# Four input projections of a hybrid convolution and linear-attention block computed as seven products of half-size blocks

## The chip, the cores and the metric

The kernel runs on one core of one Trainium2 chip. The metric is the device time of one execution in microseconds (us). A core has five engines with a queue of their own each: TensorE (PE in the profile, with its weight loads in a row of their own, PEld), VectorE (DVE), ScalarE (ACT), GpSimd (POOL) and SyncE (SP). An engine works its queue off in order. In this kernel SP issues the loads of weights and inputs, and POOL issues the small constants and everything that goes to scratch memory in DRAM and back.

## The reference

512 tokens of width 2048 pass through one layer. Only the part before the output projection is changed.

```python
u = rmsnorm(x, norm1_g)
z = u @ w_in                      # 2048 x 6160
cb, cc, ch, q, k, v, og, a_low = split(z)   # 1024 x3, 512 x2, 1024 x2, 16 columns
y_conv = group_rms(cb * causal_conv3(cc * ch)) * conv_g
log_a  = log_sigmoid(a_low @ w_gate_up + b_gate) / 16
o      = gla_chunk_causal(q, k, v, log_a)   # chunks of 64 tokens, 4 heads
y_gla  = rms(o) * gla_g * silu(og)
x = x + concat(y_conv, y_gla) @ w_out
x = x + relu(rmsnorm(x) @ w_ff1)**2 @ w_ff2
out = rmsnorm(x)
```

## The kernel before

All weights arrive in float32. For a matmul each operand is split into two rounded parts, hi and lo (ACT copies the hi part, DVE subtracts to get the lo part), and a product is the sum of three matmuls: hi by hi, hi by lo, lo by hi (`mm3`). A unit of weights is 512 KB (128 partitions by 1024 elements): SP loads it into one of four `raw` buffers, ACT makes `hi` (three buffers) and DVE makes `lo` (three buffers).

The front half runs in this order. `project_v(0)` computes half of v, 512 columns wide, token by token (`token_major`, the activations as stationary operand), while x, transposed, is loaded and split into `u` tile by tile; the square sums for the norm come from a second load of x. Two products of 264 columns (`tm_t`) give the gate's low-rank input and k. `project_v(1)` follows, with the decay gates between its matmuls, then eight products for the out-gate (`fm_og`), four for q (`fm_q`), and eight groups of the convolution, each with three products of 128 features by 512 tokens: cc, ch and cb (`fm_cc`, `fm_ch`, `fm_cb`, one call of `feature_major` each, 48 matmuls of 512 columns). The linear attention is written as a generator, `gla(h)`: a hook in `feature_major` takes one step of it after every third matmul. One chunk is a matmul `kv`, a VectorE update of the state `st`, four steps of nothing and then two matmuls `o`. A head runs in one of every two convolution groups, in its first two products.

After the front come the output projection (`tm_op`) and the two feed-forward products (`f1...` and `f...`). These two are already computed by seven products of half-size blocks: of four weight blocks `block_forms` makes seven forms by additions on DVE, each is split into hi and lo, and each product is 24 matmuls of 256 columns. A tile framework orders the instructions of each engine by a cost model of its own, and places all waits.

Of the kernel before, what the change touches and what calls it, by code (L numbers as in the profile page):

```python
# [8 lines left out]
F32 = mybir.dt.float32  # L9
# [25 lines left out]

Q0, K0, V0, O0, A0 = 3072, 3584, 4096, 5120, 6144
# [3 lines left out]
def hymba_kernel(  # L40
    ctx, tc, x, x_t, w_tok0, w_tok, w_feat, w_gate, conv_w, conv_g, g1, g2, gla_g, gf,
# [92 lines left out]
    nc.gpsimd.dma_start(glag, gla_g)  # L134
    r1 = const_tile("r1", [P, NT])
# [51 lines left out]

    u = []
    w_ready = []
    yt = [None] * KT  # L190
    with tc.tile_pool(name="mix", bufs=1) as mix:
# [4 lines left out]

        xq = [wide(f"xt_{k}", ("og0", "og1", "vv1", "kk")[k]) for k in range(4)]

        def load_u(e):
            k = 2 * e  # L200
            part = xq[k // 4][:, k % 4 : k % 4 + 2, :]
            nc.sync.dma_start(part, x_t[:, k : k + 2, :])
            for m in range(2):
                u.append(split_scaled(part[:, m, :], g1t[:, k + m : k + m + 1], "u", k + m))

        def load_first(kt):
            part = xq[0][:, kt, :]
            nc.sync.dma_start(part, x_t[:, kt, :])
            u.append(split_scaled(part, g1t[:, kt : kt + 1], "u", kt))


        ss1 = mix.tile([P, NT], F32, name="ss1", tag="ss1")
        a1 = mix.tile([P, NT], F32, name="a1", tag="a1")
        def square_sum(i):
            xi = mix.tile([P, D], F32, name=f"x_{i}", tag="yr", bufs=2)
            nc.sync.dma_start(xi, x[i * P : (i + 1) * P, :])
            S.activation(xi, xi, AF.Square, accum_out=ss1[:, i : i + 1])

        vv = [None, None]
        def project_v(n, hook, before=None):  # L220
            def put(i, b):
                if i == 0:
                    vv[n] = wide(f"vv_{n}", f"vv{n}")
                S.activation(vv[n][:, i, :], b, AF.Copy, scale=r1[:, i : i + 1])

            token_major(u, w_tok, 8 * n, 8, 512, 2, f"v{n}", put, hook, before)

        def start(j):
            if j < 7:
                load_u(j + 1)  # L230
            if 4 <= j <= 7:
                square_sum(j - 4)
            if j == 7:
                mean_eps(a1, ss1, D)
                rsqrt_of(r1, a1, mix, "r1")

        project_v(0, start, load_first)
# [10 lines left out]
        r1sb = mix.tile([P, SEQ], F32, name="r1sb", tag="r1sb")  # L248
        eab = mix.tile([P, SEQ], F32, name="eab", tag="eab")

        def along_free(dst, col, factor, name):
            b = bank(f"{name}_ps", "aux")
            for i in range(NT):
                d = mix.tile([P, P], F32, name=f"{name}_d{i}", tag="diag", bufs=1)
                V.tensor_scalar_mul(d, ident, col[:, i : i + 1])
                T.matmul(b[:, i * P : (i + 1) * P], onesg, d, start=True, stop=True)
            S.activation(dst, b, AF.Copy, scale=factor)


        alow = mix.tile([P, NT, RANK], F32, name="alow", tag="alow")  # L260
        kk = wide("kk", "kk")

        def put0(i, b):
            S.activation(alow[:, i, :], b[:, :RANK], AF.Copy, scale=r1[:, i : i + 1])
            V.tensor_scalar_mul(kk[:, i, 0:248], b[:, RANK:264], r1[:, i : i + 1])

        def put1(i, b):
            S.activation(kk[:, i, 248:512], b[:, :264], AF.Copy, scale=r1[:, i : i + 1])

        token_major(u, w_tok0, 0, 4, 264, 4, "t0", put0)  # L270
        along_free(r1b, r1, float(P), "r1b")
        along_free(eab, a1, float(P) * EPS, "eab")
        V.tensor_tensor(out=r1sb, in0=r1b, in1=r1b, op=ALU.mult)
        token_major(u, w_tok0, 4, 4, 264, 4, "t1", put1)

        kd = [kk, wide("kk_odd", "kk2")]
        G.memset(kd[1][:CHUNK], 0.0)
        al3 = mix.tile([P, NT, 96], F32R, name="al3", tag="al3")  # L280
# [33 lines left out]
        def gate_decay(i):  # L314
# [6 lines left out]
            V.tensor_tensor(out=kd[1][CHUNK:, i, :], in0=kk[CHUNK:, i, :], in1=t[CHUNK:], op=ALU.mult)  # L321
            V.tensor_tensor(out=kk[:CHUNK, i, :], in0=kk[:CHUNK, i, :], in1=t[:CHUNK], op=ALU.mult)
# [10 lines left out]
        def gates(j):  # L333
            if j == 0:
                gate_alt()
            if 1 <= j <= 2:
                gate_in(2 * j - 2)
                gate_in(2 * j - 1)
            if j == 2:
                gate_log()  # L340
            if 5 <= j <= 6:
                gate_decay(2 * j - 10)
                gate_decay(2 * j - 9)

        project_v(1, gates)


        og = [wide(f"og_{n}", f"og{n}") for n in range(2)]
        for k in range(8):
            b = feature_major(w_feat[HEADS + k], u, f"og{k}")  # L350
            t = mix.tile([P, SEQ], F32, name=f"ogt_{k}", tag=f"hs{k % 2}")
            V.tensor_tensor(out=t, in0=b, in1=r1b, op=ALU.mult)
            S.activation(og[k // 4][:, k % 4, :], t, AF.Silu)
        qt = []
        for h in range(HEADS):
            b = feature_major(w_feat[h], u, f"q{h}")
            q = mix.tile([P, SEQ], F32, name=f"q_{h}", tag=f"q{h}")
            V.scalar_tensor_tensor(
                out=q, in0=b, scalar=float(DK) ** -0.5, in1=r1b, op0=ALU.mult, op1=ALU.mult
            )  # L360
            qt.append(q)

        def gla(h):
# [3 lines left out]
            cv = slice(h % 2 * DV, (h % 2 + 1) * DV)  # L367
            for c in range(NCHUNK):
# [3 lines left out]
                    kv[:, :DV], kd[c % 2][:, i, h * DK : (h + 1) * DK], vv[h // 2][:, i, cv],  # L372
# [13 lines left out]
                for d in range(2):  # L386
                    T.matmul(
                        o[d][:, t], st[:, d * P : (d + 1) * P], qt[h][:, t], start=True, stop=True,
                        skip_group_check=True,
                    )  # L390
# [10 lines left out]
            mean_eps(a, m, 2.0)  # L401
# [15 lines left out]
        def conv(j, hook, hook_last):  # L417
            if j % 4 == 0:
                yraw.append(wide(f"y_{j}", "yr", bufs=2))
            b = feature_major(w_feat[12 + 3 * j], u, f"cc{j}", hook)  # L420
            cc = mix.tile([P, SEQ], F32, name=f"cc_{j}", tag="cc")
            V.tensor_tensor(out=cc, in0=b, in1=r1sb, op=ALU.mult)
            b = feature_major(w_feat[13 + 3 * j], u, f"ch{j}", hook)
# [5 lines left out]
            V.tensor_scalar_mul(cv, up[:, 0:SEQ], w(0))  # L429
# [4 lines left out]
            b = feature_major(w_feat[14 + 3 * j], u, f"cb{j}", hook_last)  # L434
            V.tensor_tensor(out=cv, in0=b, in1=cv, op=ALU.mult)
# [30 lines left out]

        norm = None
        for j in range(NG):
            steps = gla(j // 2) if j % 2 == 0 else iter(())
            pending = [norm]  # L470

            def hook(kt):
                if kt == 8 and pending[0]:
                    pending.pop()()
                    pending.append(None)
                next(steps, None)

            norm = conv(j, hook, y_last if j == NG - 1 else hook)
            for _ in steps:
                pass  # L480
        norm()
        y_conv(NG - 1)

# [5 lines left out]

    wt = ctx.enter_context(tc.tile_pool(name="wt", bufs=1, reuse_waits="tile"))  # L490

    def load_quarters(src, i0, n, name):

        raws = []
        for q in range(4):
            raw = wp.tile([P, UNIT], F32, name=f"raw_{name}{q}", tag="raw", bufs=RAWS)
            nc.sync.dma_start(raw[:, :n], src[i0 + q])
            raws.append(raw[:, :n])
        return raws

    def split_w(src, n, name):
        hi = wp.tile([P, UNIT], F32R, name=f"hi_{name}", tag="hi", bufs=3)
        lo = wp.tile([P, UNIT], F32R, name=f"lo_{name}", tag="lo", bufs=3)
        S.copy(hi[:, :n], src)  # L504
        V.tensor_tensor(out=lo[:, :n], in0=src, in1=hi[:, :n].bitcast(F32), op=ALU.subtract)  # L505
        return hi, lo

    def plus(in0, in1, n, name, into=None):
        w = into
        if w is None:  # L510
            w = wt.tile([P, 1024], F32, name=f"w_{name}", tag="w", bufs=2)[:, :n]
        V.tensor_tensor(out=w, in0=in0, in1=in1, op=ALU.add)  # L512
        return w

    def block_forms(src, i0, n, name):

        b12, b11, b21, b22 = load_quarters(src, i0, n, name)
        w = {}

        def parts_of(f):  # L520
            if f in (5, 6) and 1 not in w:
                w[1] = plus(b11, b12, n, f"{name}5")
                w["early"] = f == 6
            if f == 6:
                w[3] = plus(w[1], b21, n, f"{name}6", None if w["early"] else w[1])
            if f == 4:
                w[4] = plus(w[3], b22, n, f"{name}4", w[3])
# [468 lines left out]
```

## Time and profile before

| | |
|---|---|
| median of three runs | 2097.56 us (2096.71 to 2098.86) |
| the profiled execution, its own time | 2099.82 us |
| its span, first to last instruction | 2098.1 us |
| PE busy | 2060.7 us, 98% |
| weight loads busy | 1922.0 us, 92% |
| DVE busy | 1492.3 us, 71% |
| ACT busy | 884.8 us, 42% |
| mean DMA rate | 146 GB/s |

Busy time is the share in which an engine has an instruction in work. Matmuls overlap (one of 256 columns lasts 0.28 us and the next starts after less than half of that), so what a matmul costs is read from the distance of two starts and not from its length.

### The profile page before, as it was taken

To read this page: it belongs to the slowest core of one execution; us is meant where nothing else is said; L and a number is where in the kernel's file an instruction comes from. 1 tells how busy PE (TensorE), PEld (TensorE's weight loads), DVE (VectorE), ACT (ScalarE), POOL (GpSimd) and SP (SyncE) were. 2 spreads that over 40 slices of the span, in tenths; PEclk is the share of its full clock that TensorE was granted. 3 is DMA by queue.
4 is the path that set the end of the run, shared out by engine and by line. 5 is a ranking of instruction groups with operands and counts; after the bars stand their busy time and mean duration, and the time that the engine had idled before them with its cause. 6 is when DMAs were issued, how large, how long until landed. Compare 5 with 4: busy or idle time off the path is not lost. (4 is left out here: it accounts for less than half of the span.)

```text
span 2098.1 us, 34341 instructions
## 1 busy us (share of the span) xinstructions
PE 2060.7 (98%) x14408; PEld 1922.0 (92%) x14408; DVE 1492.3 (71%) x1744; ACT 884.8 (42%) x1106; POOL 133.9 (6%) x202
## 2 busy tenths in 40 slices
PE   8999999999999999999999999999999999999998
PEld 6988888888888899999999999998999999999996
DVE  5242236756754467888888888889789789888987
ACT  6242213222233334555555545555354345344343
POOL 1000000000020000000000000000000100103210
PEclk9999999999999999999999999999999999999999
DMA  7323222222253334554454454547456667667763
GB/s 295 92 80 95 96 86 86 80 81 91 82 178 117 125 91 136 165 165 151 140 164 153 147 155 147 162 158 258 132 180 205 149 163 221 162 158 237 184 187 102
DMA packets 90427, 307.11 MB, mean 146 GB/s; under 512 B 10773, under 2 KB 10821, under 8 KB 89760
## 3 DMA queue, kind: packets, MB, share of 16 engines
q1 hardware_dynamic: 69120, 242.64, 37.0%
q0 software_dynamic: 21152, 62.28, 10.6%
q8 instruction: 112, 1.84, 0.4%
q14 instruction: 43, 0.35, 0.1%
HBM read 252.19 MB, written 49.55 MB: 144 GB/s over the span
## 5 line engine op out<-in xcount | busy, mean ns | idle before, releaser
L750 PE MATMUL f<-hi_f,ah 128*128 128x256 f32 x1568 | 442.0, 282 | 10.3 <-ACT hi_f L504 5.4
L750 PE MATMUL f<-lo_f,ah 128*128 128x256 f32 x1568 | 444.0, 283 | 5.1 <-DVE lo_f L505 5.1
L750 PE MATMUL f<-hi_f,al 128*128 128x256 f32 x1568 | 441.3, 282 | 0.0
L505 DVE TENSOR_TENSOR lo_f<-w_f,hi_f 128x1024 fp32r<-128x1024 f32 (+1 forms) x256 | 304.2, 1191 | 145.6 <-ACT hi_f L504 144.0
L504 ACT CAST hi_f<-w_f 128x1024 fp32r<-128x1024 f32 (+1 forms) x256 | 261.5, 1023 | 339.0 <-PE f L750 107.0
L750 PEld LDWEIGHTS f<-hi_f,ah 128*128 128x128 f32 x1568 | 297.1, 190 | 12.4 <-ACT hi_f L504 7.0
L750 PEld LDWEIGHTS f<-lo_f,ah 128*128 128x128 f32 x1568 | 296.4, 189 | 7.7 <-DVE lo_f L505 7.1
L750 PEld LDWEIGHTS f<-hi_f,al 128*128 128x128 f32 x1568 | 297.3, 190 | 0.0
L504 ACT CAST hi_f<-raw_f 128x1024 fp32r<-128x1024 f32 (+1 forms) x192 | 196.4, 1024 | 200.3 <-PE f L750 87.1
L505 DVE TENSOR_TENSOR lo_f<-raw_f,hi_f 128x1024 fp32r<-128x1024 f32 (+1 forms) x192 | 227.8, 1187 | 26.9 <-ACT hi_f L504 26.9
L512 DVE TENSOR_TENSOR w_f<-raw_f,raw_f 128x1024 f32<-128x1024 f32 (+1 forms) x128 | 152.4, 1190 | 12.6 <-DMA raw_f<-in_w_ff 9.2
L512 DVE TENSOR_TENSOR w_f<-w_f,raw_f 128x1024 f32<-128x1024 f32 (+1 forms) x128 | 152.3, 1190 | 3.3
L656 PE MATMUL f1a<-Sh,hi_f 128*128 128x256 f32 x512 | 145.2, 284 | 0.0
L656 PE MATMUL f1c<-Sh,hi_f 128*128 128x256 f32 x512 | 144.3, 282 | 0.9 <-ACT q L679 0.9
L656 PE MATMUL f1a<-Sh,lo_f 128*128 128x256 f32 x512 | 145.1, 283 | 0.0
L656 PE MATMUL f1a<-Sl,hi_f 128*128 128x256 f32 x512 | 144.9, 283 | 0.0
L656 PE MATMUL f1c<-Sh,lo_f 128*128 128x256 f32 x512 | 144.2, 282 | 0.2 <-DVE lo_f L505 0.2
L656 PE MATMUL f1c<-Sl,hi_f 128*128 128x256 f32 x512 | 144.0, 281 | 0.0
L75 PE MATMUL tm_op<-hi_op,yh 128*128 128x512 f32 (+1 forms) x304 | 106.2, 349 | 0.0
L76 PE MATMUL tm_op<-lo_op,yh 128*128 128x512 f32 (+1 forms) x304 | 105.3, 346 | 0.0
L77 PE MATMUL tm_op<-hi_op,yl 128*128 128x512 f32 (+1 forms) x304 | 105.0, 345 | 0.0
L656 PEld LDWEIGHTS f1c<-Sh,hi_f 128*128 128x128 f32 x512 | 96.9, 189 | 1.1 <-ACT q L679 1.1
(365 smaller groups left out, 4866.8 us busy)
## 6 DMA issues: line engine op xcount, KB each, us to landing
raw_f<-in_w_ff SPq DMA_DIRECT2D x240, 512.0 KB, 3.7
a_keep<-y POOLq DMA_DIRECT2D x30, 896.0 KB, 5.1
st<-a_keep SPq DMA_DIRECT2D x49, 512.0 KB, 4.6
c_keep<-c POOLq DMA_DIRECT2D x48, 256.0 KB, 5.3
raw_op<-in_w_out SPq DMA_DIRECT2D x22, 512.0 KB, 3.6
raw_og<-in_w_feat SPq DMA_DIRECT2D x16, 512.0 KB, 3.6
raw_cc<-in_w_feat SPq DMA_DIRECT2D x16, 512.0 KB, 3.6
raw_ch<-in_w_feat SPq DMA_DIRECT2D x16, 512.0 KB, 3.7
```

What stands on the lines that cost most here:

```text
L75: T.matmul(dst, l[0], r[0], start=start, stop=False)
L76: T.matmul(dst, l[0], r[1], start=False, stop=False)
L77: T.matmul(dst, l[1], r[0], start=False, stop=stop)
L504: S.copy(hi[:, :n], src)
L505: V.tensor_tensor(out=lo[:, :n], in0=src, in1=hi[:, :n].bitcast(F32), op=ALU.subtract)
L512: V.tensor_tensor(out=w, in0=in0, in1=in1, op=ALU.add)
L656: T.matmul(dst[:, :HALF], l[:, c], r, start=start and p == m == 0, stop=p == 7 and m == 2, skip_group_check=True,)
L750: T.matmul(d, l[:, k, t], r[:, c], start=grp == k == i == e == 0, stop=grp == 1 and k == m - 1 and e == 2, skip_group_check=True,)
```

## The change

The products for v, the out-gate, q and six of the eight cb groups are now computed in the manner of the feed-forward layers: from `u` seven forms for each pair of tiles (`u_forms`), from the weights seven forms for each four blocks, seven products of 24 matmuls of 256 columns for v (per half of the rows) and for each pair of feature tiles, and additions on DVE that put the four result blocks together. Results go to scratch in DRAM by POOL's queue (`v_keep`, `og_keep`, `q_keep`, `cb_keep`) and are loaded again when they are used. The two 264-column products now come first, while `u` is loaded; the norm of x follows between the products of v; the decay gates move from the second half of v to the convolution. The linear attention no longer starts anew in every second group: gates and four heads run one behind the other as one chain of steps (`all_steps`) through cc and ch of the groups. The weights for cb of the first six groups are left out of the convolution stage, whose groups now have two products of 512 columns. The scale factor r1 is no longer applied to v, q, k and cb where they are evicted, but where the norms and gates follow. One multiplication of the convolution goes from DVE to ACT.

```diff
+        low = [[next_bank(f"tm_t{n}{i}") for i in range(NT)] for n in range(2)]
+        for j in range(4):
+            if j:
+                load_u(2 * j)
+                load_u(2 * j + 1)
+            for n in range(2):
+                h, l = unit(w_low[4 * n + j], 1056, f"t{n}_{j}", *((4, load_first) if j == n == 0 else ()))
...
+            if j:
+                u_forms(2 * j - 2)
+                u_forms(2 * j - 1)
...
+        def u_forms(p):
+
+            b = xp[p].rearrange("p a (b c) -> p (a b) c", b=2)
...
+            V.tensor_tensor(
+                out=t75, in0=b[:, 1:2, :].to_broadcast([P, 2, HALF]), in1=b[:, 0:4:3, :], op=ALU.subtract
+            )
+            V.tensor_tensor(out=t63[:, 0, :], in0=b[:, 0, :], in1=t75[:, 1, :], op=ALU.subtract)
+            V.tensor_tensor(out=t63[:, 1, :], in0=b[:, 2, :], in1=t63[:, 0, :], op=ALU.subtract)
...
+        def norm1():
+            for i in range(NT):
+                for c in range(2):
+                    xi = mb.tile([P, D // 2], F32, name=f"x_{i}{c}", tag="b4", bufs=4)
+                    nc.gpsimd.dma_start(xi, x[i * P : (i + 1) * P, c * (D // 2) : (c + 1) * (D // 2)])
+                    S.activation(xi, xi, AF.Square, accum_out=ss1[:, i, c : c + 1])
+                    yield
+            V.tensor_reduce(out=a1, in_=ss1, op=ALU.add, axis=mybir.AxisListType.X)
+            mean_eps(a1, a1, D)
+            rsqrt_of(r1, a1, mb, "r1")
...
+            def product(f, dst, start):
+                hi, lo = forms(f)
+                for p in range(KT // 2):
+                    c = slice(p * P, (p + 1) * P)
+                    sh, sl = uforms[p][f]
+                    for m, (l, r) in enumerate(((hi, sh), (hi, sl), (lo, sh))):
+                        T.matmul(
+                            dst[:, :HALF], l[:, c], r, start=start and p == m == 0,
...
+        for g in range(HEADS):
+            y = feature_pair(g, f"og{g}")
...
+            nc.gpsimd.dma_start(og_keep[g], y)
+        for g in range(2):
+            nc.gpsimd.dma_start(q_keep[g], feature_pair(HEADS + g, f"q{g}"))
+        for g in range(NCB // 2):
+            nc.gpsimd.dma_start(cb_keep[g], feature_pair(HEADS + 2 + g, f"cb{g}"))
...
+    with tc.tile_pool(name="mix", bufs=1, reuse_waits="tile") as mix:
...
+            if j < NCB:
+                cb = mix.tile([P, SEQ], F32, name=f"cb_{j}", tag="cb", bufs=2)
+                nc.gpsimd.dma_start(cb, cb_keep[j // 2][:, j % 2, :])
...
-            V.tensor_scalar_mul(cv, up[:, 0:SEQ], w(0))
+            S.activation(cv, up[:, 0:SEQ], AF.Copy, scale=w(0))
...
+        def all_steps():
+            yield from gates()
+            for h in range(HEADS):
+                yield from gla(h)
```

Two places of the new order matter for what follows. The first is ACT's queue where the 264-column products end and the first products of v begin. Before, the copies there are followed by nothing that needs a second load of x (`vv` and `kk` are evictions, `al` and `alt` belong to the gate):

```order
L70 CAST hi_t1_3_874<-raw_t1_3_873 128x1056
L70 CAST hi_v1_0_950<-raw_v1_0_949 128x1024
L70 CAST hi_v1_1_986<-raw_v1_1_985 128x1024
L268 ACTIVATE kk_449<-tm_t10_707,r1_85 128x264
L268 ACTIVATE kk_449<-tm_t11_708,r1_85 128x264
L268 ACTIVATE kk_449<-tm_t12_709,r1_85 128x264
L268 ACTIVATE kk_449<-tm_t13_710,r1_85 128x264
L70 CAST hi_v1_2_1024<-raw_v1_2_1023 128x1024
```

Now the squares of x (`x_20` to `x_31`), the root for r1 and the evictions stand between the hi parts of the second form (`hi_v003`) and the third (`hi_v002`) of v:

```order
L362 ACTIVATE x_30_982,ss1_107<-x_30_982 128x1024
L349 COPY alow_106<-tm_t03_131 128x16
L207 CAST hi_v003_793<-raw_v002_758 128x1024
L352 COPY kk_105<-tm_t10_132 128x264
L362 ACTIVATE x_31_1021,ss1_107<-x_31_1021 128x1024
L352 COPY kk_105<-tm_t11_133 128x264
L110 ACT_TABLE_LOAD
L110 ACTIVATE r1_86<-a1_108 128x4
L503 ACTIVATE alow_106<-alow_106,r1_86 128x16
L352 COPY kk_105<-tm_t12_134 128x264
L352 COPY kk_105<-tm_t13_135 128x264
L207 CAST hi_v002_824<-raw_v003_760 128x1024
```

A square waits for its load of x, a load for a buffer that an earlier square or `u_forms` gives back, and the root for DVE's sum of all eight squares; `hi_v002` is behind all of them.

The second place is where the convolution begins. Before, DVE has there the last eviction of q, the lo parts of ch and the state updates of the first head:

```order
L358 SCALAR_TENSOR_TENSOR q_3_2048<-fm_q3_1987,r1b_86 128x512
L71 TENSOR_TENSOR lo_ch0_0_2141<-raw_ch0_0_2139,hi_ch0_0_2140 128x1024
L377 COPY st_00_2065<-kv_00_2063 128x256
L379 SCALAR_TENSOR_TENSOR st_10_2083<-st_00_2065,dec_s_942,kv_10_2081 128x256
L71 TENSOR_TENSOR lo_ch0_8_2183<-raw_ch0_8_2181,hi_ch0_8_2182 128x1024
```

Now it has there the last block of cb (`y_cb2`), the square of r1 (`r1sb`), the gate's preparations and the diagonal tiles `eab_d` for a matmul of PE:

```order
L466 TENSOR_TENSOR y_cb2_3543<-e_cb2_3542,v_cb2_3695 128x256
L74 TENSOR_TENSOR lo_ch0_0_3908<-raw_ch0_0_3906,hi_ch0_0_3907 128x1024
L487 TENSOR_TENSOR r1sb_3763<-r1b_87 128x512
L491 MEMSET graw_3766 96x512
L505 MEMSET al3_3780 128x384
L255 TENSOR_SCALAR eab_d0_3814<-ident_72,a1_108 128x128
```

The tile of `r1sb` lies where `y_cb2` lay, so this instruction waits until the store of `y_cb2` to DRAM has landed, and what is behind it waits as well. PE meets the product of `eab_d0` in the middle of the first convolution product, after 27 of its 48 matmuls:

```order
L78 MATMUL fm_cc0_3795<-uh_4_424,hi_cc0_8_3855 128x512
L79 MATMUL fm_cc0_3795<-ul_4_425,hi_cc0_8_3855 128x512
L80 MATMUL fm_cc0_3795<-uh_4_424,lo_cc0_8_3856 128x512
L252 MATMUL eab_ps_3813<-eab_d0_3814,onesg_88 128x128
L78 MATMUL fm_cc0_3795<-uh_4_424,hi_cc0_8_3855 128x512
```

Here the matmul on a diagonal tile has moved from the 264-column products, where it stood before, into `fm_cc0`.

## Rows read from the trace of the kernel before

**Rows 1.** The page: span and busy time of the engines.
```profile
span 2098.1 us, 34341 instructions
...
PE 2060.7 (98%) x14408; PEld 1922.0 (92%) x14408; DVE 1492.3 (71%) x1744; ACT 884.8 (42%) x1106; POOL 133.9 (6%) x202
```

**Rows 2.** Windows: convolution stage, first and second feed-forward product, first 40 us.
```profile
core 0: us, PE busy (x) PEld busy (x) DVE busy (x) ACT busy (x) POOL busy (x), PEclk, DMA share, GB/s
288.60:588.90 300.30, 300.30 (x1366) 247.56 (x1365) 195.05 (x238) 81.09 (x100) 0.00 (x0) 1.00 0.26 83
780.00:1422.00 642.00, 640.94 (x5378) 640.53 (x5378) 529.24 (x619) 332.41 (x422) 29.07 (x32) 1.00 0.49 153
1422.00:2060.00 638.00, 620.86 (x5108) 611.77 (x5107) 543.45 (x564) 287.14 (x307) 74.74 (x111) 0.99 0.64 184
0.00:40.00 40.00, 33.34 (x129) 26.13 (x130) 22.83 (x39) 26.99 (x35) 7.02 (x16) 1.00 0.94 359
```

**Rows 3.** Waits of PE, longest first: total us, times, longest one.
```profile
PE f L750 <- DVE lo_f L505: 6.6, 13, 1.1
PE tm_v L75 <- ACT hi_v L70: 6.5, 1, 6.5
...
PE htr L566 <- DVE xr L605: 3.5, 2, 3.1
```

**Rows 4.** The tile of the out-gate's products: first and last start.
```profile
L75 PE MATMUL fm_og<-uh,hi_og x128: 389/389/401, 155.1 to 243.5; 128*128 128x512 f32 x128
...
L77 PE MATMUL fm_og<-uh,lo_og x128: 393/397/404, 155.6 to 244.0; 128*128 128x512 f32 x128
```

**Rows 5.** Timeline of PE: the same matmul in two successive feed-forward groups.
```profile
1000.44 0.28 PE L656 MATMUL f1e<-Sh,hi_f 128*128 128x256 f32 x1
...
1020.40 0.28 PE L656 MATMUL f1e<-Sh,hi_f 128*128 128x256 f32 x1
```

**Rows 6.** The page: a weight load of the first feed-forward product.
```profile
L656 PEld LDWEIGHTS f1c<-Sh,hi_f 128*128 128x128 f32 x512 | 96.9, 189 | 1.1 <-ACT q L679 1.1
```

**Rows 7.** Groups of DVE and ACT in the convolution stage.
```profile
L108 DVE RECIPROCAL crs<-crs 128x512 f32<-128x512 f32 x7 | 23.5, 3351 | 1.2 <-ACT crs L107 0.9
L71 DVE TENSOR_TENSOR lo_ch<-raw_ch,hi_ch 128x1024 fp32r<-128x1024 f32 x16 | 19.6, 1224 | 10.8 <-ACT hi_ch L70 10.7
...
L379 DVE SCALAR_TENSOR_TENSOR st<-st,dec_s,kv 128x256 f32<-128x256 f32 x28 | 13.1, 467 | 27.2 <-PE kv L371 27.2
...
L70 ACT CAST hi_cb<-raw_cb 128x1024 fp32r<-128x1024 f32 x16 | 16.8, 1049 | 69.8 <-PE fm_ch L76 38.9 <-PE fm_cc L76 26.1 <-PE fm_ch L77 4.8
```

**Rows 8.** DMA issues: KB each, median us from issue to landing.
```profile
raw_f<-in_w_ff SPq DMA_DIRECT2D x240, 512.0 KB, 3.7
a_keep<-y POOLq DMA_DIRECT2D x30, 896.0 KB, 5.1
...
xr<-in_x POOLq DMA_DIRECT2D x12, 256.0 KB, 7.1
...
graw<-in_w_gate POOLq DMA_DIRECT2D x3, 34.0 KB, 6.5
```

**Rows 9.** Windows of PE after its longest wait before the feed-forward.
```profile
780.00:782.00 2.00, 2.00 (x10) 0.50 0.18 66
782.00:784.00 2.00, 2.00 (x11) 0.50 0.00 0
784.00:786.00 2.00, 2.00 (x16) 0.80 0.00 0
```

**Rows 10.** Timeline of the start: first split of u, first matmul.
```profile
5.23 0.72 ACT L94 ACTIVATE uh<-xt,g1t 128x512 fp32r<-128x512 f32 x1 [2.64 <-DMA g1t<-in_g]
...
6.51 0.80 PE L75 MATMUL tm_v<-hi_v,uh 128*128 128x512 f32 x1 [6.51 <-ACT hi_v L70]
```

**Rows 11.** Timeline of ACT: the root for r1 and its table load.
```profile
44.76 1.28 ACT L107 ACT_TABLE_LOAD   x1
46.06 0.20 ACT L107 ACTIVATE r<-a 128x4 f32<-128x4 f32 x1
```

More of the change, by code (lines that the diff above doesn't have):

```diff
@@ new lines, in plus, with block_forms, parts_of @@
+    def plus(in0, in1, n, name, into=None):
+        w = into
+        if w is None:
+            w = sums[-1].tile([P, 1024], F32, name=f"w_{name}", tag="w", bufs=2)[:, :n]
+        V.tensor_tensor(out=w, in0=in0, in1=in1, op=ALU.add)
+        return w
+    def block_forms(src, i0, n, name):
+        b12, b11, b21, b22 = load_quarters(src, i0, n, name)
+        w = {}
+        def parts_of(f):
+            if f in (5, 6) and 1 not in w:
+                w[1] = plus(b11, b12, n, f"{name}5")
+                w["early"] = f == 6
+            if f == 6:
+                w[3] = plus(w[1], b21, n, f"{name}6", None if w["early"] else w[1])
+            if f == 4:
+                w[4] = plus(w[3], b22, n, f"{name}4", w[3])
+            if f == 7:
+                w[7] = plus(b11, b21, n, f"{name}7")
+            v = {1: b12, 3: b21, 2: b22, 5: w.get(1), 6: w.get(3), 4: w.get(4), 7: w.get(7)}[f]
+            return split_w(v, n, f"{name}{f}")
+        return parts_of
@@ L206, in load_first @@
[L206 to L235, printed above, removed]
@@ L245, in hymba_kernel @@
         V.tensor_tensor(out=g3[32:64], in0=graw[32:64], in1=g3[32:64].bitcast(F32), op=ALU.subtract)
[L248 to L274, printed above, removed]
         kd = [kk, wide("kk_odd", "kk2")]
         G.memset(kd[1][:CHUNK], 0.0)
+        for i in range(NT):
+            S.activation(alow[:, i, :], alow[:, i, :], AF.Copy, scale=r1[:, i : i + 1])
         al3 = mix.tile([P, NT, 96], F32R, name="al3", tag="al3")
@@ L488, in hymba_kernel @@
     c_keep = [[tc.dram_tile([P, 2, HALF], F32, name=f"c_keep{n}{q}") for q in range(4)] for n in range(4)]
[L490 to L527, printed above, removed]
-            if f == 7:
-                w[7] = plus(b11, b21, n, f"{name}7")
-            v = {1: b12, 3: b21, 2: b22, 5: w.get(1), 6: w.get(3), 4: w.get(4), 7: w.get(7)}[f]
-            return split_w(v, n, f"{name}{f}")
-        return parts_of
+    sums.append(ctx.enter_context(tc.tile_pool(name="wt", bufs=1, reuse_waits="tile")))
     hf = ctx.enter_context(tc.tile_pool(name="hf", bufs=1))
```

308 lines of the change are left out of this document (247 added, 61 removed).

## The prediction

> **What bounds the kernel now.** The page comes first: PE is busy 98% of the span, 2060.7 of 2098.1 us, DVE 71%, ACT less [rows 1]. An engine that is busy because its neighbours make it wait would look different, so the second view is the waits of PE: the longest is the first hi part of the weights at the start, 6.5 us, and all other entries belong to the output projection and the feed-forward products [rows 3]. Between the first matmuls and the output projection PE waits for nobody. The windows say the same by stage: in 300.3 us of the convolution PE is busy for all of them, DVE for 195, the DMA engines for 0.26 of their time at 83 GB/s; in the start the same engines moved 359 GB/s [rows 2]. So the time of the front half is the number of its matmuls times their distance, and a change of it is worth what it takes from that product, less the waits that it makes.
>
> The distance comes from starts. The 384 matmuls of the out-gate, 512 columns each, start between 155.1 and 244.0 us [rows 4]: 88.9 / 383 = 0.2321 us. A feed-forward group of 7 x 24 matmuls of 256 columns returns after 1020.40 - 1000.44 = 19.96 us [rows 5]: 19.96 / 168 = 0.1188 us, everything between the products included. Two half-width matmuls thus take 0.2376 us where one full one takes 0.2321, 2.4% more.
>
> **The change: matmuls of PE, -30 us.** Removed are 384 matmuls of 512 columns for v, 384 for the out-gate, 192 for q and 6 x 48 = 288 for cb, together 1248; at 0.2321 us that is 289.7 us. Added are seven products of 24 for each block group: v has four such groups (672 matmuls), out-gate four (672), q two (336), cb three (504), together 2184 of 256 columns; at 0.1188 us 259.5 us. The difference is -30.2 us. It is the eighth that the method saves (36 us) less the 2.4%. The 264-column products, the `kv`, `o` and gate matmuls only move.
>
> At the distance one rule speaks against the change. The Trainium skill ("TensorE: Matmul & The Clock Gate", section "Back-to-back issue gap") gives 81 ns for sustained pairs of weight load and matmul at 128 columns and 131 ns at 512, so halving the width would not halve the time; an estimate from that page at 256 columns, on the line between, is 98 ns, and the sum 2184 x 0.098 - 1248 x 0.131 = +51 us. This trace has 232 and 119 ns, so the measurement decides, and the term stays -30.
>
> **Start, +1 (0 to 3).** The first matmul now belongs to `tm_t` and comes after the first hi and lo parts, as before at 6.51 us, with the first split of `u` at 5.23 [rows 10]. Its first step wants two units, `w_low` for two columns of the product, before PE can work without gaps, and DMA is full there anyway (0.94) [rows 2]. Below: DMA-bound in both, 0. Above: one more unit at 3.7 us [rows 8], part of it covered, so 3.
>
> **Entry of v, +6 (1 to 12).** While the 264-column products run (384 matmuls at an estimated 0.122 us, on the line between the two measured widths, 47 us), DVE makes the lo parts of `u` and of the weights and `u_forms`. Then it needs for each product of v additions on weights and lo parts at 1.224 us each [rows 7], with only two products (2 x 24 x 0.1188 = 5.7 us) ready ahead. In ACT's queue between `hi_v003` and `hi_v002` stand the squares, the evictions and the root. A square waits for its load, a load of x by POOL takes 7.1 us in a burst [rows 8], and the loads wait for buffers from squares before. The last square (estimated 1 us, as the cast of the same width, 1.049 [rows 7]), DVE's sum, the table load of 1.28 and the root [rows 11] come to some 3 us behind the last landing, four evictions of 264 columns to 2 us more, and the third product follows only then: the last loads' 7.1 + 3 + 2 + 1.05 + 1.22 = 14.4 us, of which 5.7 are covered by products at hand and some by loads issued earlier. If none of these is issued early, 9 to 10 are lost; if the loads are in before `u_forms` end, 1 (the lo part itself). I take the middle, 5, since the loads are free to go as soon as buffers are, but the buffers are shared with `u_forms`. A gap of 3.1 us before `htr` [rows 3] was followed by a granted clock of 0.50 for about 5 us, the lower of the two levels, 1.2 against 2.4 GHz [rows 9]: in these 5 us PE lost about 2.4. A wait here of that length carries the same price; I add half of it, 1, to the middle, which makes **+6**.
>
> By the Trainium skill ("ScalarE: Activation LUTs", section "What ACT_TABLE_LOAD costs") a table load of 1283 ns is followed by a drain of about 1380 ns, which would lengthen this chain by 1.4 us. Here the load took 1.28 and the root started 0.02 us later [rows 11], so no drain is added.
>
> **Handover to convolution and gates, +4 (0 to 8).** `r1sb` takes the place of `y_cb2` and waits until its store has landed; POOL's stores to scratch take 5.1 us [rows 8]. Behind it on DVE are a memset, `al3` and `eab_d0`, with `r1sb` some 1536 elements in a row, at 1.224 us per 1024 about 1.8. The last block's additions (0.47 [rows 7]) are ahead. So `eab_d0` is there 7.4 us after the last product of cb or a little later, while PE has 27 x 0.2321 = 6.3 us of work before it wants it: 1 to 2 us. The gate's weights `graw` are loaded behind the memset, 6.5 us [rows 8], and the gate's logarithm costs two table loads (1.28 each) and two passes of ACT; each has three full-width matmuls of cover per step, so about 1 us each is left of them. Below: all covered, 0. Above: store, load and logarithm end one behind the other, 8.
>
> **State steps of linear attention, +1 (0 to 12).** The 32 chunk steps are now one chain. Each goes `kv` on PE, `st` on DVE (0.467 [rows 7]), `o` on PE some 15 matmuls later, 3.5 us. DVE's work in the stage stays near 190 us (six lo pairs of cb, `cv` and the evictions leave, 12 lo parts at 1.224 and some others; the gates come), while the stage shrinks by 288 x 0.2321 = 67 us to some 235: 80% busy in place of 65%. `st` waits behind what DVE has in work; only the reciprocal of 3.35 us [rows 7] reaches 3.5. Eleven or twelve of those fall in this stage and a collision costs at most 1 us, hence 12 above; nothing waited there before, hence 0 below; I take 1.
>
> **Block forms, +1 (0 to 7).** Per feature pair DVE has 11 passes of 1.22 us, some five of 0.47 and for the out-gate 1.2 more, 15.8 to 17 of 19.96 us. The same form of work has 529 us of DVE in 642 us (82%) in the first feed-forward product and PE without wait but for 1.1 us; in the second, with 85%, 17.1 of 638 us are idle [rows 2]. On 259 us that is 0.4 to 7; the nearer row is the first.
>
> **Costs at nothing.** The results written to scratch and read again are about 6.5 MB each way; the DMA engines work 0.26 to 0.64 of the time in these stages and can do 359 GB/s [rows 2], so 13 MB are 36 us of their time in 500. If that cover were gone, four first uses would wait for a load, 4 x 5.1 = 20 us. The scaling by r1 at new places, `cv` on ACT (42% busy [rows 1]) and the longer life of `u` put nothing on PE.
>
> **The sum.** -30 + 1 + 6 + 4 + 1 + 1 = -17. The profiled execution has 2099.8 us of its own, 1.7 more than its span and 2.3 above the median of 2097.56. So the sum stands for 2082.8 there, and for **2080.5** beside the median.
>
> **The rivals.** First, the waits hide altogether: entry 1, handover 1, all else nothing, about -27 and 2070 (2067 to 2073). For it speaks that PE waited nowhere in the front half [rows 3]; against it, that the root and the squares now stand ahead of weights that PE needs. Second, entry, handover and block forms are at their upper bounds, -30 + 10 (without the clock) + 8 + 5 = -7 and 2090 (2088 to 2094). For it speaks the second feed-forward product, where DVE at 85% makes PE wait for lo parts [rows 2, 3]. Third, slower: the chain of state steps sets the pace. If each `st` finds one lo pass ahead of it that its cover doesn't hold, 32 x 1.22 = 39 us are lost, -17 + 39 = +22 and 2120. It decides the sign from 17 / 32 = 0.53 us a step, and a slowdown that can be told from 0.66. Against it: in the 28 `st` updates of the shown stage the idle time ahead, 27.2 us, was all for `kv`, which came last, and not for DVE [rows 7], and 3.5 us of cover are more than two lo passes. Fourth, the half-width matmuls don't come at 0.1188 us. Their weight load lasts 189 ns [rows 6]; if it did not overlap, 2184 x 0.189 = 412.8 us, +123 in place of -30, 2204 with no waits. The break-even distance is 289.7 / 2184 = 0.1326 us; the feed-forward products, which have such loads, are at 0.1188, and at 638 / 5108 = 0.1249 in the second with all its waits [rows 2], so this is nearly excluded. Last, several terms near their tops take the gain: within 0.2%.
>
> **How the numbers follow.** A measurement tells this kernel from no change at about 0.2%, 4.2 us. Chances: the forecast with 2073 to 2088, 0.52; waits hidden 0.16; upper bounds 0.16; within 0.2% 0.06; slower 0.06 (state chain 0.05, distance 0.01); below 2067, 0.04. Faster is 0.52 + 0.16 + 0.16 + 0.04 = 0.88. The range takes the forecast and its two neighbours, 2068 (all lower bounds: -30.2 + 1 = -29) to 2094, and leaves out 0.17.
>
> **What the profile after would show.** Right: 1248 matmuls fewer of 512 columns and 2184 more of 256, at 0.119 us within v, `og`, `q` and `cb`; a wait of PE for `hi_v002` or `lo_v002` of some us, one for `eab_d0` of 1 to 2, others under 1. The stage from the start of v to the end of the convolution shortens by 30 less these waits. Wrong: if `st` or `o` stand high among the waits of PE the third rival is at work; if PE's clock falls to 0.5 in several places, the waits cost more than their lengths; if DVE or the `lo` parts of `og` and `cb` end most waits, the block forms are dearer than in the feed-forward; if the distance within a product isn't 0.119, the first term fails.

## The result, and the profile after

The changed kernel takes 2082.73 us in the median of six executions (2079.15 to 2089.12) beside 2097.91 for the kernel before (six executions, 2096.71 to 2099.07). The ratio is 0.993 with a 95% interval of 0.9912 to 0.9949: 15 us less, where 17 were forecast (2080.5, range 2068 to 2094). Run again later it took 2083.85 (five executions), ratio 0.9925 (0.9912 to 0.9939). The profiled execution has 2085.04 us of its own and a span of 2083.3, 14.8 under that of before [rows 1].

The page of the changed kernel, span and busy time of the engines:

```profile
span 2083.3 us, 36658 instructions
...
PE 2036.1 (98%) x15344; PEld 1950.0 (94%) x15344; DVE 1637.9 (79%) x1916; ACT 951.6 (46%) x1213; POOL 157.1 (8%) x245
```

PE has 936 matmuls more and is busy 25 us less; its share is still 98%, DVE's rose from 71 to 79%. The output projection's first matmuls (`hi_ready`) start at 573.0 us, before at 589.5. So the front half is 16.5 us shorter. Behind it, where nothing was changed, this profile is 1.7 us longer; in the profiles of all kernels here that part takes 1505.5 to 1513.8 us (1508.6 before), so this is no effect that can be told from its own variation. Windows of the changed kernel by stage (264-column products, v, out-gate, q, cb by blocks, convolution; columns as in [rows 2], the two figures ahead of DMA's rate are PE's granted clock and the DMA share):

```profile
6.30:55.80 49.50, 49.50 (x384) 49.33 (x385) 44.00 (x69) 42.26 (x71) 4.25 (x8) 1.00 0.83 294
55.80:138.70 82.90, 80.80 (x682) 80.40 (x681) 65.03 (x71) 35.74 (x44) 3.80 (x7) 1.00 0.36 122
138.70:219.00 80.30, 80.30 (x674) 80.30 (x673) 64.18 (x68) 36.77 (x44) 2.15 (x4) 1.00 0.40 133
219.00:259.10 40.10, 40.10 (x338) 40.10 (x337) 31.34 (x34) 17.27 (x21) 1.07 (x2) 1.00 0.39 130
259.10:319.30 60.20, 60.20 (x506) 60.20 (x505) 42.69 (x46) 24.49 (x30) 1.60 (x3) 1.00 0.38 125
319.30:573.00 253.70, 247.28 (x1136) 204.12 (x1135) 193.48 (x249) 92.14 (x121) 15.60 (x27) 0.98 0.32 105
```

The three stages of feature pairs have no idle time of PE at all: 80.3 + 40.1 + 60.2 = 180.6 us for 672 + 336 + 504 = 1512 matmuls, 0.1194 us each, where the feed-forward gave 0.1188 [rows 5]. v has 2.1 us of idle time, the convolution 6.4, and only the convolution has a granted clock below 1. The waits of PE by what released them (total us, times, longest), without those of the start and behind the output projection:

```profile
PE eab_ps L252 <- DVE al L507: 3.4, 1, 3.4
PE o L616 <- DVE oy L638: 1.7, 1, 1.7
PE v L397 <- ACT hi_v L207: 1.2, 1, 1.2
PE dec L554 <- DVE ls L536: 0.9, 1, 0.9
PE v L397 <- DVE lo_v L208: 0.9, 1, 0.9
...
PE fm_cc L80 <- DVE lo_cc L74: 0.4, 1, 0.4
```

Before, no wait between the first matmuls and the output projection stood in that view [rows 3]. The timeline shows what the longest one is. The last block of cb, its store, `r1sb` and the matmul of `eab_d0`:

```profile
319.52 0.42 DVE L466 TENSOR_TENSOR y_cb<-e_cb,v_cb 128x256 f32<-128x256 f32 x1 [0.67 <-PE e_cb L438]
320.82 0.53 POOL L479 DMA_DIRECT2D cb_keep<-y_cb  x1 [19.33 <-ACT hi_ch L73]
327.34 0.69 DVE L487 TENSOR_TENSOR r1sb<-r1b 128x512 f32<-128x512 f32 x1 [5.63 <-DMA cb_keep<-y_cb]
329.11 0.49 PE L252 MATMUL eab_ps<-eab_d,onesg 128*128 128x128 f32 x2 [3.38 <-DVE al L507]
```

DVE stands idle for 5.63 us at `r1sb` until the store has landed, 6.4 us after its issue; 1.8 us later PE gets `eab_d0`, as worked out, but the store took longer than the 5.1 us of [rows 8], although those stores are larger (896 KB; this one has 512). The view names the last instruction ahead (`al`); the cause is two links further back, on the DMA. Windows of the changed kernel behind this wait and behind the one for `ls` (PEclk is the third figure from the end):

```profile
328.00:330.00 2.00, 0.89 (x5) 0.74 (x6) 1.92 (x7) 0.39 (x2) 1.14 (x3) 0.95 0.00 0
330.00:332.00 2.00, 2.00 (x6) 1.61 (x5) 0.68 (x3) 0.00 (x0) 2.00 (x4) 0.50 0.45 106
332.00:334.00 2.00, 2.00 (x11) 1.58 (x10) 0.58 (x3) 0.49 (x1) 2.00 (x5) 0.70 0.89 246
...
350.00:352.00 2.00, 2.00 (x8) 1.57 (x6) 1.02 (x2) 1.19 (x2) 0.04 (x1) 0.57 0.88 279
352.00:354.00 2.00, 2.00 (x11) 1.90 (x10) 0.00 (x0) 0.71 (x1) 0.00 (x0) 0.50 0.99 401
354.00:356.00 2.00, 2.00 (x6) 1.61 (x5) 1.26 (x2) 1.36 (x2) 0.00 (x0) 0.50 0.27 107
356.00:358.00 2.00, 2.00 (x8) 1.54 (x8) 1.97 (x4) 1.09 (x3) 0.52 (x1) 0.72 0.01 4
```

Each wait was followed by a stretch at the lower of the two levels. One minus the clock, times the length, gives an estimate of what it cost: 1.7 us behind the first and 3.4 behind the second. 6.4 us of waits and about 5 of half clock are what the convolution lost by this estimate; the version without them, below, is 10.8 us shorter there.

### The profile page after: what moved, and what is told of

Same layout as the page of the kernel before. It is cut to its first block, busy times and chain, and to the rows that moved or that the text cites. A ratio compares the mean times of both kernels' runs of the same rounds, so it can differ in the third digit from the quotient of the medians.

```text
span 2083.3 us, 36658 instructions
## 1 busy us (share of the span) xinstructions
PE 2036.1 (98%) x15344; PEld 1950.0 (94%) x15344; DVE 1637.9 (79%) x1916; ACT 951.6 (46%) x1213; POOL 157.1 (8%) x245
```

## The experiments

The kernel before ran beside each of three groups of experiments, and the ratios below are against it: 2098.47 us beside the first four (nine executions), 2099.61 beside the next four (nine), 2099.70 beside the last three (seven). The changed kernel itself ran again only beside the second group. The intervals of the single edits overlap that of the changed kernel (0.9912 to 0.9949), so for them the stages and waits of the profiles decide, and not the medians.

**The store at the handover.** A tile that is written late, the convolution's output, is placed first in the pool, so that it and not `r1sb` lies where `y_cb2` lay.

```diff
+        yraw = [wide("y_0", "yr", bufs=2)]
         r1sb = mix.tile([P, SEQ], F32, name="r1sb", tag="r1sb")
...
-        yraw = []
...
-            if j % 4 == 0:
+            if j == 4:
                 yraw.append(wide(f"y_{j}", "yr", bufs=2))
```

> The tile of the convolution's output is placed first in the pool, so that r1sb, graw and the gate's tiles no longer lie where y_cb2 lay and wait for no store. My theory: the changed kernel lost 3.4 us of waiting there and about 2 us more in the 4 us of half clock that followed (329.1 to 333.3 us), so this gives about 2082.7 - 5.4 = 2077.3 us, no wait of PE for eab_ps, and a granted clock of 1.00 from 324 to 340 us. Rival: the load of the gate's weights (6.5 us behind the memset) is late next, PE waits for the gate's product instead, and the time stays within 2081 to 2084.

Measured: 2080.47 us (2077.59 to 2082.67), ratio 0.9909 (0.9894 to 0.9924). The wait for `eab_ps` is gone, the clock is 1.00 from 324 to 340, and the convolution took 247.3 us in place of 253.7, 6.4 less. Of these the edit accounts for about 5.1, the wait of 3.4 and the 1.7 of half clock behind it; the rest is the clock elsewhere, which behind `dec` didn't fall this time (3.4 us less) and behind `o` did (1.7 more). The load of the gate's weights makes nobody wait, so the rival's mechanism falls, though the time came out between the two forecasts (2077.3 and 2081 to 2084). Between the two profiled executions the front half is 5.0 us shorter, with 2.3 us more in v (85.2 for 82.9), and what lies behind it 2.0 us longer. The waits of PE and two windows of this kernel:

```profile
PE v L397 <- ACT hi_v L207: 2.0, 1, 2.0
...
PE v L397 <- DVE lo_v L208: 0.9, 1, 0.9
```

```profile
64.00:68.00 4.00, 3.99 (x22) 4.00 (x23) 3.93 (x4) 0.59 (x1) 0.00 (x0) 0.62 0.16 33
...
324.00:328.00 4.00, 4.00 (x20) 3.33 (x19) 1.45 (x6) 1.34 (x3) 4.00 (x8) 1.00 0.86 252
...
448.00:452.00 4.00, 4.00 (x16) 3.25 (x15) 3.50 (x5) 0.00 (x0) 0.00 (x0) 0.67 0.61 188
```

Here the clock fell after the wait of v and after that of `o`; in the changed kernel's first profile both waits (2.1 and 1.7 us) passed without it.

**The gate's logarithm.**

```diff
-            yield from (None,) * 14
+            yield from (None,) * 20
```

> Six more empty steps between the gate's logarithm and the decays (20 in place of 14, that is 18 full matmuls or 4.2 us more cover). My theory: the wait of PE for ls (0.9 us) and the half clock behind it (350 to 357 us in the changed kernel, about 3 us lost) both go: about 2082.7 - 4 = 2078.7. Rival: the clock falls because of the 32 matmuls of two columns (dec) and not because of the wait; then only 0.9 us go, 2081.8, and a stretch with the clock at 0.5 stands again where dec is.

Measured: 2078.15 us (2076.07 to 2079.72), ratio 0.9901 (0.9887 to 0.9914). The wait for `ls` and the half clock behind it are gone, and the wait of `o` for `oy` as well, since the heads moved against the convolution. The convolution took 247.8 us although `eab_ps` waited 3.6. The waits of PE ahead of the output projection, without that of the start, and the windows with the matmuls for `dec`, which start at 349.6 us:

```profile
PE eab_ps L252 <- DVE al L507: 3.6, 1, 3.6
PE v L397 <- DVE lo_v L208: 0.9, 1, 0.9
...
PE v L397 <- ACT hi_v L207: 0.3, 1, 0.3
```

```profile
348.00:352.00 4.00, 3.92 (x22) 3.06 (x21) 3.58 (x5) 3.25 (x5) 0.80 (x2) 1.00 0.75 265
352.00:356.00 4.00, 4.00 (x24) 3.39 (x23) 3.36 (x5) 1.59 (x3) 0.94 (x2) 1.00 0.68 261
```

The same 32 matmuls of two columns run at full clock when nothing waits ahead of them. One profile alone doesn't refute the rival, since with the wait the clock stays up in some profiles as well. But over these matmuls it stayed at 1.00 in all four profiles without the wait (this one, the two with all edits, and cb by full products without the waits) and fell in four of the eight with it, so the rival is unlikely.

**The root.**

```diff
-            S.activation(alow[:, i, :], alow[:, i, :], AF.Copy, scale=r1[:, i : i + 1])
+            V.tensor_scalar_mul(alow[:, i, :], alow[:, i, :], r1[:, i : i + 1])
```

> The scaling of the gate's low-rank input by r1 goes from ACT to DVE, so that ACT's copies and the third hi part of v no longer stand behind DVE's Newton step. My theory: hi_v002 comes 1.5 us earlier and PE's waits at hi_v002 and lo_v002, 1.2 and 0.9 us, nearly go: about 2081, with no clock change. Rival: lo_v002 is held up by DVE's own chain or by the load of the weights, and the 2 us stay.

Measured: 2079.41 us (2076.85 to 2081.32), ratio 0.9907 (0.9893 to 0.992). v took 80.4 us without any wait, 2.5 less. ACT's timeline of the changed kernel and of this one shows the step:

```profile
59.36 0.21 ACT L110 ACTIVATE r<-a 128x4 f32<-128x4 f32 x1
60.46 0.31 ACT L503 ACTIVATE alow<-alow,r 128x16 f32<-128x16 f32 x1 [0.90 <-DVE r L114]
60.67 0.36 ACT L352 COPY kk<-tm_t 128x264 f32<-128x264 f32 x1
60.93 0.70 ACT L503 ACTIVATE alow<-alow,r 128x16 f32<-128x16 f32 x3
61.54 0.36 ACT L352 COPY kk<-tm_t 128x264 f32<-128x264 f32 x1
61.80 1.05 ACT L207 CAST hi_v<-raw_v 128x1024 fp32r<-128x1024 f32 x1
```

```profile
58.22 0.20 ACT L110 ACTIVATE r<-a 128x4 f32<-128x4 f32 x1
58.33 0.64 ACT L352 COPY kk<-tm_t 128x264 f32<-128x264 f32 x2
58.86 1.06 ACT L207 CAST hi_v<-raw_v 128x1024 fp32r<-128x1024 f32 x1
```

From the root to the third hi part it is 2.44 us in the one and 0.64 in the other: the squares, the table load and the root were in time; four scalings of 16 columns, which wait for DVE's Newton step, were what came too late. The waits at the entry of v vary without this edit too (1.2 us with the edit on the logarithm, 2.9 with that on the store), so how much of the 2.5 us the edit gives in each execution isn't shown. In this kernel the store of `y_cb2` landed sooner as well (`eab_ps` waited 0.9 us), which is not owed to the edit.

**cb by full products.** `NCB = 6` becomes `NCB = 0`.

> All eight cb groups are computed by products of 512 columns in the convolution again; v, out-gate and q stay as changed. My theory: PE's distance alone prices this part: 288 x 0.2321 - 504 x 0.1194 = 66.8 - 60.2 = +6.7 us, and the wait at the handover stays (behind the store of the last q in place of the last cb): 2089.4. Rival: the denser stage of the convolution (DVE at 80%) costs as much as cb by blocks saves, so that with cb moved back the time stays at 2081 to 2085.

Measured: 2082.80 us (2078.20 to 2085.46), ratio 0.9922 (0.991 to 0.9935), the changed kernel's own time. I was wrong that the wait at the handover stays: with three feature pairs fewer, `r1sb` starts at 260.1 us without a wait, 2.1 us before the last store of q lands (262.3), so it doesn't lie on that tile, and PE has no wait for `eab_ps` in this profile. The waits of `o` for `oy` and of `fm_cc` are gone as well. From the first matmul of cb or of the convolution to the output projection the two profiles take 313.1 us here and 60.2 + 253.7 = 313.9 in the changed kernel. So cb by blocks gained its matmuls there, and the waits that came with it took as much, 5.1 us at the handover with its half clock and 2.1 at `o` and behind. That the dense stage was to blame, as the rival had it, isn't shown by that; the same edit without the waits, below, takes it up.

**The changed kernel again, all edits together, and two loads.** The second kernel has the three edits above and five more empty steps between two heads, so that `o` of the next head doesn't wait for `oy` to free its bank:

```diff
                 V.tensor_tensor(out=g, in0=t, in1=g, op=ALU.mult)
-            yield
+            yield from (None,) * 6
```

> The changed kernel itself, on the chip of the next three, as their measure: 2079 to 2089 us, 2082 in the middle. If the spread of its executions comes from the granted clock, which falls after some of the waits in some executions only, its profile shows the waits eab_ps, o, dec and hi_v002 again (3.4, 1.7, 0.9, 1.2 us), but not the same stretches of half clock.

> The three edits so far together (first tile of the pool, six more steps behind the logarithm, the scaling by r1 on DVE), and five more empty steps between two heads of the linear attention. My theory, that waits and half clocks are all that stands between the changed kernel and its sum of matmuls: stages of 80.4 us for v and 242 us for the convolution in place of 82.9 and 253.7, no wait of PE over 0.9 us ahead of the output projection, no half clock there, and 2070 to 2073 us with a spread below that of the changed kernel. Rival: a wait that is taken away comes back elsewhere (the next load or DVE is late); then 2077 to 2079 as with one edit alone.

Measured: the changed kernel 2083.85 us (2080.47 to 2085.69); with all edits 2073.91 (2072.80 to 2074.57), ratio 0.9879 (0.9865 to 0.9892), and 2073.42 (2071.83 to 2073.99), ratio 0.9875 (0.986 to 0.9889) when run once more. This is 9.9 us below the changed kernel beside it, the intervals are clear of each other, and it is up to 1 us above the 2070 to 2073 that were expected. Its eight executions lie within 2.7 us, the eleven of the changed kernel within 10. Windows of the version with all edits (v, out-gate and q, cb, convolution):

```profile
56.60:136.90 80.30, 80.30 (x682) 80.28 (x681) 64.39 (x74) 33.99 (x38) 3.80 (x7) 1.00 0.36 123
136.90:257.30 120.40, 120.40 (x1010) 120.40 (x1009) 95.54 (x101) 54.05 (x65) 3.21 (x6) 1.00 0.38 132
257.30:317.50 60.20, 60.20 (x506) 60.20 (x505) 42.66 (x46) 24.49 (x30) 1.60 (x3) 1.00 0.36 125
317.50:560.40 242.90, 242.80 (x1136) 199.92 (x1135) 191.84 (x249) 92.11 (x121) 15.52 (x27) 1.00 0.33 109
```

Behind the start no wait and no half clock are left in the front half of this profile, and the convolution is 10.8 us shorter than in the changed kernel's first, with the same 1136 matmuls. (The second profile of this version has one wait, 0.6 us for `lo_v002`, and no half clock either.) Nothing came back elsewhere; the rival falls. The output projection starts at 560.4 us, 29.1 earlier than in the kernel before (28.3 in the second profile), about what the matmuls alone give. What the five steps between the heads add isn't shown apart: the edit on the logarithm alone had removed the wait of `o` too.

The changed kernel's second profile gave the waits `o`, `dec` and `hi_v002` again (1.7, 0.9, 0.8 us), but `eab_ps` waited 1.1 us in place of 3.4, since the store landed 4.1 us after its issue. Behind that wait and those of v and `o` the clock stayed at 1.00; behind that of `dec` it fell (0.64 from 344 to 348 us, 0.51 from 348 to 352).

One part undone: the first tap of the convolution on DVE again.

```diff
-            S.activation(cv, up[:, 0:SEQ], AF.Copy, scale=w(0))
+            V.tensor_scalar_mul(cv, up[:, 0:SEQ], w(0))
```

> One part undone: the first tap of the convolution goes back from ACT to DVE, 8 x 0.488 = 3.9 us of work in a stage of 254 us in which DVE is busy 76%. My theory: DVE isn't what PE waits for there, so 0, 2080 to 2085 as the changed kernel in this call. Rival, the dense stage: state updates and lo parts come later, and most of the 3.9 us show, together with new waits of PE for st or lo_cc.

Measured: 2084.40 us (2082.93 to 2085.11), ratio 0.9928 (0.9915 to 0.9942); the changed kernel beside it 2083.85. The edit on ACT is worth nothing that can be measured. Of the rival a trace is there: `o` waits 0.4 us for `st` once, the only such wait seen, and 2.2 us for `oy` in place of 1.7. The convolution took 249.7 us beside 250.0 in the changed kernel's second profile, so most of the 3.9 us don't show.

DVE's load raised in the block products:

```diff
+            for _ in range(3 if g < 6 else 0):
+                V.tensor_tensor(out=y, in0=y, in1=y, op=ALU.max)
             return y
```

> One suspected cost raised: three more passes of DVE over the result (maximum of a tile with itself, 1.22 us each, which changes no value) in each of the four feature pairs of the out-gate and the two of q. DVE goes from 80% to 98% there. My theory of the margin: PE doesn't wait until DVE is full, at most 3 us of waits for lo_og, lo_q (and none of half clock), 2081 to 2087. Rival, the block forms at the edge already (as in the second feed-forward product, 85% and 17 us idle): of 22 us of added work 10 or more show, 2092 and above.

Measured: 2087.11 us (2082.05 to 2089.14), ratio 0.9938 (0.9922 to 0.9955). The stages with the added passes, out-gate and q, in this kernel:

```profile
140.10:220.40 80.30, 80.30 (x675) 80.30 (x674) 71.91 (x77) 37.11 (x44) 2.15 (x4) 1.00 0.38 129
220.40:260.50 40.10, 40.10 (x338) 40.10 (x338) 37.25 (x40) 17.38 (x21) 1.06 (x2) 1.00 0.42 139
```

Neither stage is 0.1 us longer. DVE went to 90 and 93% and not to 98, as part of the passes was placed later. The median is just past the upper end of my range. This profile is 5.4 us longer than that of the changed kernel beside it, 1.6 of them in v and 2.8 in the convolution, where it has half clocks that the other doesn't have and waits 1.4 us more for the store, and 0.8 at the start. So block products on DVE had room for passes of 1.22 us, and the rival falls.

**cb by full products, without the waits.** The version with all edits and `NCB = 0`, beside that version itself.

> The version with all the edits once more, as the measure of the next: 2073 to 2075 us on a chip on which the kernel before takes 2098 to 2100.

> All eight cb groups by products of 512 columns again, but now with the waits of the handover, the logarithm, the root and between heads taken away. By the distance of the matmuls cb by blocks is worth 288 x 0.2321 - 504 x 0.1194 = 6.7 us. My theory: where the waits are gone on both sides, this shows whole, 2080 to 2081, that is 6 to 7 us above the version with all edits. Rival: the price of cb by blocks isn't in the matmuls' distance, or the denser stage costs as much; then it is less than 3 us above.

Measured: 2076.62 us (2074.16 to 2079.18), ratio 0.9895 (0.9879 to 0.9912), against 2073.42: 3.2 us, between the two theories. By stage, from the first matmul of cb or of the convolution to the output projection, it is 309.2 us against 60.2 + 243.0 = 303.2, that is 6.0 us, near the 6.7 of the matmuls. The windows of the version with all edits (cb, convolution) and of this one:

```profile
257.90:318.10 60.20, 60.20 (x506) 60.20 (x506) 42.71 (x46) 24.49 (x30) 1.60 (x3) 1.00 0.37 125
318.10:561.10 243.00, 242.91 (x1136) 200.16 (x1135) 191.80 (x249) 92.09 (x121) 15.50 (x27) 1.00 0.33 109
```

```profile
256.10:565.30 309.20, 309.13 (x1424) 254.65 (x1423) 210.39 (x261) 101.89 (x131) 12.33 (x21) 1.00 0.31 101
```

The profile gives some of it back in stages whose code is the same in both (each of start, v, output projection and first feed-forward product was 0.7 to 0.9 us shorter in this profile; in v it is the 0.6 us that the other waits for `lo_v002`). The price in the stage is shown; why the whole differs by less, 2.4 us in the profiled spans, stays open.

**The state steps.**

```diff
                         in1=kv[:, :DV], op0=ALU.mult, op1=ALU.add,
                     )
+                V.tensor_tensor(out=st, in0=st, in1=st, op=ALU.max)
                 state[0] = st
```

> The changed kernel with one pass more of DVE on the path of each state step of the linear attention: the maximum of st with itself, an estimated 0.42 us, which changes no value, so that the 32 links of the chain take twice as long on DVE. My theory: other matmuls stand between kv and o, and PE waits for no st: within 3 us of the changed kernel, 2082 to 2086 where the kernel before takes 2099. The rival that the chain sets the pace: 32 x 0.42 = 13 us more, 2096 and above, with o or kv high among the waits of PE.

Measured: 2080.97 us (2078.21 to 2083.56), ratio 0.9912 (0.9897 to 0.9926). The added pass took 0.415 us, 32 times, and PE waited for no `st`:

```profile
L612 DVE TENSOR_TENSOR st<-st 128x256 f32<-128x256 f32 x32 | 13.3, 415 | 0.3
```

The time is 1 us below my range and not 13 above the changed kernel's. The rival that was to turn the sign has no hold: other matmuls stand between `kv` and `o`.

## Why the prediction was right, step by step

It was right in sign, in total and in the main mechanism, fewer matmul microseconds less a few waits. Two terms were off in opposite ways, the entry of v 3.4 us too high and the handover 5 too low in the profiled execution, so that the total came within 2.2 us of the median is in part luck. And one of its own signs of being wrong came true: the clock fell to 0.5 in two places, and the waits cost more than their lengths.

- **Matmuls and block forms, -30 and +1.** 2184 at the measured 0.1194 us are 260.8 us, against 289.7 removed: -28.9, both terms together. The front half without waits confirms it, 29.1 and 28.3 us shorter than that of the kernel before. No wait in out-gate, q and cb; DVE at 71 to 80% there, and with 90 to 93% still none. The Trainium skill's sustained spacing ("TensorE: Matmul & The Clock Gate", section "Back-to-back issue gap"), an estimated 98 ns at this width, is not met: the rows have 119.4 ns.
- **Start, +1.** 3.0 us of matmuls are missing in the first 40 us (254 starts, where 33.7 us at 0.1211 us each hold 278), and before 3.5 were (129 where 33.5 us hold 144 [rows 2]): nothing lost, and 0.5 us gained.
- **Entry of v, +6.** Measured 2.6 us (82.9 against 80.3 without waits), at `hi_v002` and `lo_v002` as forecast. The chain was sized by loads of x that come last; the loads and squares were early (the last square began at 56.62 us, 0.8 after the first matmul of v), and what remained was the Newton step ahead of the scalings on ACT. The Trainium skill adds a drain of about 1380 ns to a table load ("ScalarE: Activation LUTs", section "What ACT_TABLE_LOAD costs"). It is not in this trace either: the load took 1.28 us and the root started 0.02 later. The extra 1 for half clock was not drawn in this profile; in that of the first experiment it was, 2.0 + 0.9 us of waits and a window at 0.62.
- **Handover and gates, +4.** This is the term that was too small in the profiled execution. The waits were 3.4 (`eab_ps`, 1 to 2 forecast) and 0.9 us (`dec`, about 1 forecast), with an estimated 1.7 and 3.4 of half clock behind them: 9.4 us, past its upper bound of 8. In the second profile of the same kernel they are 1.1 + 0.9 + 3.4 = 5.4 us, inside the bounds; the store and the clock decide. Half clock had been counted for v alone. The step that failed is thus the one that gave the price of half clock only to a wait of 3 us at one place. That `dec` came out as forecast is luck: the prediction set three matmuls of cover against each part of the gate's logarithm. In the trace the whole of it (two table loads, two passes of 1.9 us, DVE's 2.3) takes 8.8 us from its first table load at 339.92 to `dec` at 348.74, and PE had 37 other matmuls to do meanwhile, about 8.6 us.
- **State steps, +1.** 1.7 us, not for `st` but for a bank that `oy` still read. The cover of 15 matmuls isn't what stands in the trace: between the last matmul of `kv` and its first `o` there are 6 to 77 others, where the kernel before has 12 to 14. The cover held, at one step only just (`st` ends at 433.06 us, its `o` starts at 433.30).
- **Costs at nothing.** The scratch traffic cost nothing in transfer, at a DMA share of 0.32 to 0.40; it cost through one store that something else had to wait for.
- **Slips in the sums.** The fourth rival's 2204 adds its 123 us to the forecast; added to the median before they give 2221. The first rival's terms give -28 and not -27, and the chain at the entry of v leaves 8.7 us and not 9 to 10. None of them moves the forecast.

Front half: -28.9 for the matmuls, 2.6 in v, 10.8 in the convolution and -0.5 at the start are -16.0, beside -16.5 measured from the two traces. The waits at the entry of v, at `eab_d0` and behind the gate's logarithm were found where they were predicted; that of `o` for `oy` was not foreseen, and the one forecast for the block forms did not come. Taking the waits away gave 10 us more, to 2073.4 and 2073.9. This is just above the range that the prediction gave the case in which the waits hide (2070, range 2067 to 2073).

## What to carry to other kernels

When work moves so that a tile's first writer meets a store to DRAM that still reads the same memory, the wait doesn't show as a transfer but as an engine that another engine waits for: follow the chain two links back, and give that memory to a tile which is written late. Price a wait of TensorE at its length plus a stretch of half clock that may follow (an estimated 1.7 or 3.4 us here, behind a wait of 0.9 us in half of the profiles), at every place and not only at the longest. Where a gain of 1% is spread over a long stage, compare stages between two fixed instructions, since one median can hide it behind waits that come and go.

## What the runs showed of the hardware

Whether the clock falls behind a wait is not decided by its length alone. Behind the 0.9 us at `dec` it fell in four profiles (the changed kernel in both, cb by full products, and DVE's load raised) and stayed at 1.00 in four (the handover, the root, the tap on DVE, the state steps). Behind the 1.7 us at `o` it fell in two (the handover, the root) and not in three; behind 2.2 and 0.4 us there it fell with the tap on DVE. At the entry of v it fell behind 1.7 us with DVE's load raised (a window at 0.58), behind 2.0 us with the state steps and behind 2.9 at the handover, and it stayed up behind 1.7 and 2.1 us in the two profiles of the changed kernel. All three waits of `eab_ps` of 2.5 us and more (2.5, 3.4, 3.6) were followed by a fall, and the four of 0.9 to 1.2 us were not. Each of these falls cost an estimated 1.7 or 3.4 us.

The spread of the changed kernel goes with the granted clock. Of its eleven executions the five with a mean clock of 0.994 or 0.995 took 2080.9 us on average, the three with 0.993 2083.8 and the three with 0.991 or 0.992 2087.2; a thousandth of the clock is 2.1 us here, so falls that come in some executions only account for most of it. At which places they fell is known for the two profiled executions alone, and the waits themselves vary too.

The store of the last 512-KB tile of cb to scratch landed 3.9 to 6.8 us after its issue in ten profiles. In the seven in which `r1sb` waits for it, the wait of `eab_ps` was this time less 3.0 us in each (0.9 us behind 3.9, 3.6 behind 6.6), so the store alone moved it. The store ahead of it, of the same size on the same queue, took 2.9 us in all ten. What delays the last one was not tested.
